# Weight tiles of three opening groups parked or subtracted on VectorE, the state decay on ScalarE, and parking during a down projection

## The chip, the cores and the metric

The kernel runs on one core of one Trainium2 chip. The metric is device time in microseconds: 1893.84 us, the median of three runs (1893.59 to 1896.18). TensorE is called PE below, VectorE DVE, ScalarE ACT, GpSimd POOL, and SyncE, which issues the DMAs, SP.

## The reference

One inference step of a two-layer decoder for a prompt of 512 tokens and a sample group of 8 sequences of one token each, 520 tokens together, width 1024, all in float32:

```python
m = hybrid_mixer(rmsnorm(x, norm_mix_pre[0]), ...)   # layer 0: dilated attention and an SSD scan
m = gdn_mixer(rmsnorm(x, norm_mix_pre[1]), ...)      # layer 1: gated DeltaNet
x = x + rmsnorm(m, norm_mix_post[l])
f = swiglu(rmsnorm(x, norm_ffn_pre[l]), w_gate, w_up, w_down)   # (silu(h @ w_gate) * (h @ w_up)) @ w_down
x = x + rmsnorm(f, norm_ffn_post[l])
```

The DeltaNet input weight has 48 column tiles of 128 (tiles 0 to 7 are q, 8 to 15 k, 16 to 31 v, 32 to 47 z) and 32 more columns for two gates. The FFN has 2816 hidden columns, 22 tiles. For each sample sequence and each of 16 heads DeltaNet also returns the new state `s * g + outer(k, u)`, a 128 x 128 matrix.

## The kernel before

Activations lie transposed, features on partitions and the 520 tokens along the free dimension, in two halves of 256 and 264. A float32 product is made of three matmuls per k-tile and half: high part of the weight with high part of the activation, the same with the activation's low part, and the weight's low part with the activation's high part (`lin`, L327). `WStream.split` (L172) makes the two parts of a unit of four k-tiles by 128 columns: a cast of the raw weights gives `whi`, on ACT (L317) or, at every `hi_v`th unit, on DVE (L318), and raw less high gives `wlo` (L193), on POOL at every `lo_pool`th unit and on DVE otherwise. `lo_pool = 1` puts all on POOL, 0 none. Raw weights come in loads of 1 MB, 256 columns of eight k-tiles or 128 columns of sixteen, into two buffers; `whi` and `wlo` have four each.

While the first FFN runs its gate and up tiles, units of the DeltaNet weight are **parked**: `park` (L152) loads a unit of 256 KB, casts it on ACT, subtracts on POOL and stores the low part to DRAM, each call doing one of these steps for three successive units. Later `split` fetches a parked low part by DMA (`wlo<-pk`) and subtracts nothing; the high part is cast again. The list (`PTILES`) holds tiles 10 to 15, 0 to 7 and 16 to 21, forty units, and there are forty calls, two to a pair of tiles for the gate and two for the up, from pair 1 on; two more calls drain the last units.

Each stage ends in `out_proj` (L497): eight output tiles, the last ones by halves. Then the residual and the norm of the new activations go half by half: for each of eight feature tiles DVE multiplies the mixer's output with R (L302, tiles `p` or `bm`), adds it to the residual stream, and ACT and DVE make the high part (`Hh`; in DeltaNet `Hl`) and the low part (`Hl`; in DeltaNet `bm`, L309) of the scaled sum. So that PE has work as soon as half 0 of a feature tile is there, the next stage opens with `group` (L336): several column tiles at once, half 0 first. In the FFNs these are gate tiles 0 and 1 and up tiles 0 and 1, eight units of which the up tiles' lie outside the rings (`p` in the first, `b` and `cs` in the second); in DeltaNet the 32 gate columns, tile 8 and tile 9 (in `cs`). `out_proj` leaves `lo_pool = 1`, so POOL makes these low parts.

In the second FFN, between the tiles, `state_steps` (L1867) updates the sample's states, four heads at a time in 32 steps: SP loads a state of 128 x 512 into `cs` and a broadcast row `b<-ud`, POOL multiplies it by its decays (L302, `cs<-cs,small`), DVE adds the outer product in two instructions (L309, `cs<-b,CS,cs`), and two steps on SP stores it. A pair of tiles takes four steps, beginning with pair 1. In that stage DVE multiplies the gate's sums by the norm (`sq<-acc,R`), ACT applies Silu (into `acc` or `small`), DVE multiplies with the up tile (`sq<-acc` or `sq<-small,acc`), ACT casts the product and DVE makes its low part. `sq` has three buffers, the accumulators four.

The program text gives what is issued; a scheduler settles each engine's order, in which loads and casts of weights and evictions have high priority, and engines and DMA queue then work strictly in that order.

Of the kernel before, what the change touches and what calls it, by code (L numbers as in the profile page):

```python
# [13 lines left out]
ALU = mybir.AluOpType  # L14
# [13 lines left out]
KF = FF // 128  # L28
# [90 lines left out]
 'yd': 'G'}  # L119


PTILES = [*range(10, 16), *range(8), *range(16, 22)]


def KN(n, v, *others):
# [6 lines left out]
class WStream:  # L132
# [19 lines left out]
    def park(s, ins):  # L152

        k = s.k
        with k.tc.issue_after(ins), k.tc.issue_after(k.last_load):
            done, new = s.wait
            s.wait = [None, None]
            if done:
                d = k.dr.tile([128, 4, 128], F32, tag="pk%d" % len(s.parked), name="pk%d" % len(s.parked))
                k.dma(d, done[2].bitcast(F32))  # L160
                s.parked[done[0]] = d
            if new:
                k.cp("A", new[2], new[1])
                k.tt(new[2], new[1], new[2].bitcast(F32), ALU.subtract, k.nc.gpsimd)
                s.wait[0] = new
            if s.todo:
                ap, c0, k0 = s.todo.pop(0)
                q = len(s.todo) % 2
                raw, lo = k.B("cs", 1040 + 512 * q, 4, 128), k.B("b4", 2080 + 512 * q, 4, 128, dt=F32R)
                k.dma(raw, ap[k0 * 128:(k0 + 4) * 128, c0:c0 + 128].rearrange("(k p) c -> p k c", p=128))  # L170
                s.wait[1] = (ap.tensor.name, ap.offset, c0, k0), raw, lo
# [37 lines left out]
            for j in range(4):  # L209
                yield kts[k0] + j, hi[:, j], lo[:, j]  # L210

    def rows(s, ap, c0, loads):

        for k0, n, offs in loads:
            raw = s.load(ap, k0, n, c0, 128)
            for o in offs:
                m = min(4, n - o)
                hi, lo = s.split(raw, o, m, 0)
                for j in range(m):
                    yield k0 + o + j, hi[:, j], lo[:, j]  # L220


class Ker:
# [112 lines left out]
    def group(s, w, xh, xl, nkt):  # L336

        w = [list(v) for v in w]
        ps = [{} for _ in w]
        for t in range(len(w)):  # L340
            if t % 2 == 0:
                a = s.acc()
            ps[t][0] = a[:, 256 * (t % 2):256 * (t % 2) + 256]
        for t in range(len(w)):
            ps[t][1] = (s.acc() if t < 2 else s.mx())[:, 0:HW[1]]
        for h in (0, 1):
            for t, v in enumerate(w):
                s.lin(v, xh, xl, nkt, (h,), ps[t])
        return ps

    def lnexp(s, ins):
# [145 lines left out]
    def out_proj(s, rows, xh, xl, nkt, mp, n, l, pre, tail=2, final=False):  # L497

        s.mp, s.sqs = mp, ([], [])
        if not final:  # L500
            tail = KN("tail%d%d" % (n, l), tail, 2, 3, 4)

        def evac(ps, ot):
            ins = None
            with s.tc.high_priority():
                for h in ps:
                    if ot == 7:
                        s.sqs[h].append(s.tms(HW[h]))
                        ins = s.act(s.sqs[h][0], ps[h], AF.Square)
                    if ot == 7 and final and h:  # L510
                        s.ts(mp[:, ot, HALF[h]], ps[h], s.gain(n, l, ot))
                    else:
                        s.act(mp[:, ot, HALF[h]], ps[h], scale=s.gain(n, l, ot))
                    if ot < 7:
                        s.add_sq(h, ps[h], ot == 0, s.tmp)
            return ins

        for ot in range(8 - tail):
            evac(s.lin(rows(ot), xh, xl, nkt), ot)
            if final and ot == 2:  # L520
                s.final_early()
        s.lo_pool = KN("lp_t%d%d" % (n, l), 2, 1, 3, 4)
        for h in (0, 1):
            for ot in range(8 - tail, 8):
                ins = evac(s.lin(rows(ot), xh, xl, nkt, (h,)), ot)
            if h == 0:
                with s.tc.issue_after(ins):
                    s.nc.scalar.preload_act_table_set("natural_log_exp_and_others")
                if final:
                    s.final_first()  # L530
                else:
                    s.pre = pre()
                    s.prenorm(*s.pre, 0, s.residual(n == 3, 0))
        if final:
            s.final_last()
        s.lo_pool, s.hi_v = 1, 0

    def spill(s):
        s.xd = s.dr.tile([128, KD * NT], F32, tag="xd", name="xd", bufs=2)
# [547 lines left out]
    def ffn(s, l):  # L1087
        nc = s.nc
        g, u, d = s.i["w_ffn_gate"][l], s.i["w_ffn_up"][l], s.i["w_ffn_down"][l]
        order = ["b4", "p0", "X", "p7"] + (["bm", "p2"] if l == 0 else ["p2", "bm"])  # L1090
        s.gen(*(("b4", "p0") if l == 0 else ("b4", "cs")))
        x = s.lay("Hh"), s.lay("Hl")

        def hid(w):
            def f(k, h):
                sl = 2 * k + w
                if sl < 4:
                    return s.B("b4", sl * NT, NT, dt=F32R)[:, HALF[h]]
                n, sl = order[1 + (sl - 4) // 8], (sl - 4) % 8
                return s.layh(n)(sl, h)  # L1100
            return f

        hh, hl = hid(0), hid(1)
        spare = lambda on: {h: s.mx("ma")[:, 0:HW[h]] for h in (0, 1)} if on else None
        kts = list(range(8))
        ax = [("p0", 1024 * q) for q in range(4)] if l == 0 else [("b4", 0), ("b4", 1024), ("b4", 2048), ("cs", 1040)]
        first = s.group([s.W.tile(g, 128 * t, kts) for t in (0, 1)] +
                        [s.W.tile(u, 128 * t, kts, out=ax[2 * t:2 * t + 2]) for t in (0, 1)], *x, 8)
        s.gen("p2" if l == 0 else "bm")
        if l == 0:  # L1110
            w = s.i["w_gdn_in"][0]
            s.copy_every = 0
            s.W.todo = [(w, 128 * t, k0) for t in PTILES for k0 in (0, 4)]
        s.lo_pool = KN("lp_f%d" % l, 1, 2, 3)
        s.hi_v = KN("hv_f%d" % l, 0, 2, 3, 4, 1)
        if l:
            s.gen("cs")
            s.new_small()
            sgs = s.small(NT)
            states = s.state_steps()  # L1120
        for p in range(11):
            sg = {}
            for t in (2 * p, 2 * p + 1):
                ps = first[t] if p == 0 else s.lin(s.W.tile(g, 128 * t, kts), *x, 8, ps=spare(t < 2 + KN("ma_f%d" % l, 0, 1, 2)))
                for h in (0, 1):
                    sl = (s.B("cs", NT * (t % 2), NT) if l == 0 else sgs if t % 2 else s.accT)[:, HALF[h]]
                    gt = s.tmp(HW[h])
                    with s.tc.high_priority():
                        s.tt(gt, ps[h], s.R2[:, HALF[h]], ALU.mult)
                    with s.tc.issue_after(s.norm_ins):  # L1130
                        ins = s.act(sl, gt, AF.Silu)
                    sg[t, h] = sl
                if l == 0 and p:
                    s.W.park(ins)
                if l and p:
                    next(states, None)
            for t in (2 * p, 2 * p + 1):
                ps = first[2 + t] if 2 + t < len(first) else s.lin(s.W.tile(u, 128 * t, kts), *x, 8)
                for h in (0, 1):
                    gt = s.tmp(HW[h])  # L1140
                    with s.tc.high_priority():
                        s.tt(gt, sg[t, h], ps[h], ALU.mult)
                    a = hh(t, h)
                    ins = s.act(a, gt)
                    s.tt(hl(t, h), gt, a.bitcast(F32), ALU.subtract)
                if l == 0 and p:
                    s.W.park(ins)
                if l and p:
                    next(states, None)
        for _ in states if l else ():  # L1150
            pass
        while l == 0 and s.W.wait != [None, None]:
            s.W.park(ins)
        s.gen("Hh")
        s.lo_pool = KN("lp_d%d" % l, 1, 2, 3)
        s.hi_v = KN("hv_d%d" % l, 0, 2, 3, 4, 1)
        s.out_proj(lambda ot: s.W.rows(d, ot * 128, [(0, 16, (0, 4, 8, 12)), (16, 6, (0, 4))]), hh, hl, KF,
                   s.B("Hh", 0, KD, NT), 3, l, lambda: (0, 1, s.lay("Hl"), s.layh("bm")), final=l == 1)

    def cache_shift(s):  # L1160
# [706 lines left out]
    def state_steps(s):  # L1867

        i, o = s.i, s.o
        dap = lambda d: d if isinstance(d, bass.AP) else d[:]  # L1870
        ud = dap(s.ud)
        gb = s.small(8, 2, 16)
# [5 lines left out]
        for n in range(4 * NS + 2):  # L1878
            with s.tc.issue_after(s.last_load):
                if n > 1:  # L1880
                    s.dma(state(o["sgs"], n - 2), S(n - 2))
                if 0 < n < 4 * NS + 1:
                    t, (b, h) = S(n - 1), at(n - 1)
                    s.tt(t, t, gb[:, b, 0, h].unsqueeze(2).to_broadcast([128, 4, 128]), ALU.mult, s.nc.gpsimd)
                    for j in range(2):
                        v = slice(2 * j, 2 * j + 2)
                        s.stt(t[:, v], ub(n - 1)[:, v], s.kqs[:, h.start // 2 + j, b, 0:1], t[:, v], ALU.mult, ALU.add)
                if n < 4 * NS:
                    b, h = at(n)
# [51 lines left out]
```

## Time and profile before

| | |
|---|---|
| median of three runs | 1893.84 us |
| profiled execution | 1886.62 us, its span 1884.8 us, 1.8 us around it |
| PE / DVE / POOL / ACT busy | 1744.3 / 1160.9 / 890.8 / 769.3 us |
| mean granted PE clock | 0.966 |
| first FFN: opening; gate, up and down | 434 to 475; to 803 |
| last tiles of the first down projection, by halves | 803 to 845 |
| DeltaNet: opening; body; z and output projection | 845 to 900; to 1300; to 1440 |
| second FFN: opening; with state steps; rest and down | 1440 to 1521; to 1670; to 1783 |
| end | 1783 to 1884.8 |

Times inside the span are of that one profiled execution, which was 7.2 us shorter than the median. A row of a timeline has start, duration, engine, line, operation, output<-inputs, shape, count, and in square brackets how long the engine was idle before it and what ended that. A row of the table of windows has the stretch and its length, then busy time and instruction count of PE, weight loads, DVE, ACT and POOL, the granted clock, the DMA engines' busy share and GB/s.

### The profile page before, as it was taken

What the parts mean: (1) busy time and instruction counts of PE and PEld (TensorE: products, weight loads), DVE (VectorE), ACT (ScalarE), POOL (GpSimd) and SP (SyncE); (2) the same over time, 40 slices, a digit from 0 to 9 for tenths busy, and PEclk for the clock granted to TensorE, in tenths of its full rate; (3) what the DMA queues carried; (4) which work ended last, traced back from release to release, by engine and by line L of the source; (5) the groups of instructions that cost most, each with busy time, mean ns of one, the idle gap of its engine ahead of it and who ended that gap; (6) DMA issues with size and microseconds to landing.
All of it is one profiled execution on the core that took longest, in us unless ns stands there. A gap on an engine that the chain in (4) does not pass through costs nothing.

```text
span 1884.8 us, 36666 instructions
## 1 busy us (share of the span) xinstructions
PE 1744.3 (93%) x14263; PEld 1656.7 (88%) x14263; DVE 1160.9 (62%) x2325; ACT 769.3 (41%) x1868; POOL 890.8 (47%) x793
## 2 busy tenths in 40 slices
PE   7889999898999999989977888989999999999996
PEld 6878777598999999978977887888998999999995
DVE  6898879539433331168799967788703866753025
ACT  5432235555433333346765655644435311111222
POOL 2565657234666663342342564544557333323452
PEclk9999999898999999999988999999999999999998
DMA  7336766354556553346753113246435588863554
GB/s 258 129 126 184 221 193 179 130 154 126 157 182 189 185 175 100 92 141 212 245 172 112 43 45 110 60 125 186 135 91 180 160 257 262 262 206 123 160 160 152
DMA packets 328784, 300.39 MB, mean 159 GB/s; under 512 B 14529, under 2 KB 299910, under 8 KB 327442
## 3 DMA queue, kind: packets, MB, share of 16 engines
q1 hardware_dynamic: 327958, 297.37, 50.7%
q8 instruction: 112, 1.84, 0.4%
q10 hardware_dynamic: 652, 0.68, 0.1%
q14 instruction: 62, 0.51, 0.1%
HBM read 261.98 MB, written 72.52 MB: 177 GB/s over the span
## 4 chain that ended last, share of the span: by engine, by line
PE 50%; DVE 18%; DMA 9%; ACT 4%; issue 4%; POOL 2%; SPq 1%; DVEq 0%; ACTq 0%; POOLq 0%
PE acc L296 43%; PE ma L296 4%; DVE p L302 3%; DVE cs L309 3%; PE mb L296 2%; DMA b<-ud 2%; DMA raw<-in_w_ffn_down_dram 1%; DVE wlo L193 1%; ACT L312 1%; DMA cs<-in_state_gdn_dram 1%; POOL cs L302 1%; SPq L324 1%; DVE b L302 1%; DVE Hl L309 1%; PE mb L299 1%
## 5 line engine op out<-in xcount | busy, mean ns | idle before, releaser
L193 POOL TENSOR_TENSOR wlo<-raw,whi 128x512 fp32r<-128x512 f32 (+2 forms) x342 | 453.2, 1328 | 504.9 <-ACT whi L317 304.3
L296 PE MATMUL acc<-Hl,whi 128*128 128x256 f32 (+1 forms) x2576 | 561.4, 291 | 29.7 <-DVE cs L302 18.1
L296 PEld LDWEIGHTS acc<-Hl,whi 128*128 128x128 f32 x2576 | 419.2, 193 | 43.8 <-issue 18.8
L317 ACT CAST whi<-raw 128x512 fp32r<-128x512 f32 (+3 forms) x392 | 234.3, 603 | 436.2 <-PE acc L296 335.5
L296 PE MATMUL acc<-Hh,whi 128*128 128x256 f32 (+1 forms) x1824 | 390.2, 289 | 9.6 <-DVE sq L302 6.3
L296 PE MATMUL acc<-Hh,wlo 128*128 128x256 f32 (+1 forms) x1824 | 389.7, 289 | 1.2 <-DVE wlo L193 1.2
L296 PEld LDWEIGHTS acc<-Hh,whi 128*128 128x128 f32 x1824 | 293.6, 192 | 17.2 <-DVE sq L302 9.2
L296 PEld LDWEIGHTS acc<-Hh,wlo 128*128 128x128 f32 x1824 | 293.4, 192 | 9.0 <-issue 6.7
L296 PE MATMUL acc<-bm,whi 128*128 128x256 f32 (+1 forms) x1136 | 234.8, 290 | 0.1
L296 PE MATMUL acc<-p,whi 128*128 128x264 f32 (+1 forms) x1280 | 226.4, 284 | 0.0
L193 DVE TENSOR_TENSOR wlo<-raw,whi 128x512 fp32r<-128x512 f32 (+1 forms) x141 | 117.6, 835 | 140.3 <-ACT whi L317 137.7
L296 PEld LDWEIGHTS acc<-p,whi 128*128 128x128 f32 x1280 | 187.8, 190 | 0.8 <-DVE p L302 0.5
L296 PEld LDWEIGHTS acc<-bm,whi 128*128 128x128 f32 x1136 | 181.1, 193 | 2.8 <-issue 2.1
L318 DVE CAST whi<-raw 128x512 fp32r<-128x512 f32 x131 | 65.4, 503 | 179.8 <-PE acc L296 136.4
L296 PE MATMUL acc<-Hl,wlo 128*128 128x256 f32 (+1 forms) x752 | 169.7, 295 | 1.2 <-DMA wlo<-pk 0.7
L296 PE MATMUL acc<-p,wlo 128*128 128x256 f32 (+1 forms) x704 | 162.0, 284 | 7.1 <-DVE wlo L193 7.1
L296 PEld LDWEIGHTS acc<-Hl,wlo 128*128 128x128 f32 x752 | 126.1, 196 | 3.9 <-issue 1.6
L296 PEld LDWEIGHTS acc<-p,wlo 128*128 128x128 f32 x704 | 117.4, 189 | 8.0 <-DVE wlo L193 7.9
L296 PE MATMUL acc<-X,whi 128*128 128x264 f32 (+1 forms) x512 | 99.1, 288 | 1.1 <-ACT X L312 1.1
L309 DVE SCALAR_TENSOR_TENSOR cs<-cs,cw 128x512 f32<-128x512 f32 x100 | 90.4, 905 | 12.0 <-POOL cs L302 7.0
L302 POOL TENSOR_TENSOR cs<-cs,small 128x512 f32<-128x512 f32 x48 | 55.1, 1152 | 87.8 <-DMA cs<-in_state_gdn_dram 68.8
L296 PEld LDWEIGHTS acc<-X,whi 128*128 128x128 f32 x512 | 79.3, 193 | 2.4 <-ACT X L312 2.2
(466 smaller groups left out, 2989.6 us busy)
## 6 DMA issues: line engine op xcount, KB each, us to landing
raw<-in_w_gdn_in_dram SPq DMA_DIRECT2D x24, 1024.0 KB
raw<-in_w_ffn_gate_dram SPq DMA_DIRECT2D x22, 1024.0 KB
raw<-in_w_ffn_up_dram SPq DMA_DIRECT2D x22, 1024.0 KB
raw<-in_w_ffn_down_dram SPq DMA_DIRECT2D x20, 1024.0 KB
raw<-in_w_hyb_in_dram SPq DMA_DIRECT2D x16, 1024.0 KB
out_sv_dram<-in_cache_attn_v_dram SPq DMA_DIRECT2D x16, 1023.0 KB
out_sk_dram<-in_cache_attn_k_dram SPq DMA_DIRECT2D x16, 1023.0 KB
cs<-in_w_gdn_in_dram SPq DMA_DIRECT2D x40, 256.0 KB
```

What stands on the lines that cost most here:

```text
L193: eng.tensor_tensor(out=lo[:, :nk, d:d + n], in0=raw[:, :, o:o + n], in1=hi[:, :nk, d:d + n].bitcast(F32), op=ALU.subtract)
L296: s.nc.tensor.matmul(out, lhsT=lhsT, rhs=rhs, start=start, stop=stop, skip_group_check=skip)
L299: s.nc.tensor.transpose(out, in_, s.ident[0:in_.shape[0], 0:in_.shape[0]])
L302: return (eng or s.nc.vector).tensor_tensor(out=out, in0=a, in1=b, op=op).ins
L309: return s.nc.vector.scalar_tensor_tensor(out=out, in0=a, scalar=sc, in1=b, op0=op0, op1=op1).ins
L312: return s.nc.scalar.activation(out=out, in_=in_, func=f, **kw).ins
L317: return s.nc.scalar.copy(out, in_).ins
L318: return (s.nc.vector if e == "V" else s.nc.gpsimd).tensor_copy(out, in_).ins
L324: return (eng or s.nc.sync).dma_start(out=out, in_=in_).ins
```

## The change

Five things change. The list of parked units becomes tiles 8 to 15 and 0 to 7 of the DeltaNet weight, then gate tiles 0 and 1 and up tiles 0 and 1 of the second FFN, then tiles 16 to 22 of DeltaNet: 54 units. The forty calls in the first FFN's gate and up take the first forty; the last 14 and the draining are done in the first down projection, where `rows` calls `park` three times per output tile. `out_proj` leaves `lo_pool = 0`, so low parts of an opening group that are not parked are made by DVE. `group` takes half 1 k-tile by k-tile over all column tiles instead of column tile after column tile. The state steps begin with pair 2 of the second FFN. The decay of a state step is done by ACT in four instructions of 128 x 128, each with the head's decay as its scale.

```diff
-PTILES = [*range(10, 16), *range(8), *range(16, 22)]
+PTILES = [*range(8, 16), *range(8)]
+DTILES = [*range(16, 23)]
...
     def park(s, ins):
 
         k = s.k
-        with k.tc.issue_after(ins), k.tc.issue_after(k.last_load):
+        with k.after(ins), k.tc.issue_after(k.last_load):
...
-    def rows(s, ap, c0, loads):
+    def rows(s, ap, c0, loads, steps=False):
...
                 for j in range(m):
                     yield k0 + o + j, hi[:, j], lo[:, j]
+                if steps and o % 8 == 4:
+                    s.park(None)
...
-        for h in (0, 1):
+        for t, v in enumerate(w):
+            s.lin(v, xh, xl, nkt, (0,), ps[t])
+        for n in range(nkt):
             for t, v in enumerate(w):
-                s.lin(v, xh, xl, nkt, (h,), ps[t])
+                kt, hi, lo = v[n]
+                for lhs, x, st, sp in ((hi, xh, n == 0, False), (hi, xl, False, False), (lo, xh, False, n == nkt - 1)):
+                    s.mm(ps[t][1], lhs, x(kt, 1), st, sp)
...
-        s.lo_pool, s.hi_v = 1, 0
+        s.lo_pool, s.hi_v = 0, 0
...
-            s.W.todo = [(w, 128 * t, k0) for t in PTILES for k0 in (0, 4)]
+            s.W.todo = ([(w, 128 * t, k0) for t in PTILES for k0 in (0, 4)] +
+                        [(s.i[n][1], 128 * t, k0) for n in ("w_ffn_gate", "w_ffn_up") for t in (0, 1) for k0 in (0, 4)] +
+                        [(w, 128 * t, k0) for t in DTILES for k0 in (0, 4)])
...
-                if l and p:
+                if l and p > 1:
                     next(states, None)
...
-        while l == 0 and s.W.wait != [None, None]:
-            s.W.park(ins)
...
-        s.out_proj(lambda ot: s.W.rows(d, ot * 128, [(0, 16, (0, 4, 8, 12)), (16, 6, (0, 4))]), hh, hl, KF,
+        s.out_proj(lambda ot: s.W.rows(d, ot * 128, [(0, 16, (0, 4, 8, 12)), (16, 6, (0, 4))], l == 0 and ot < 6), hh, hl, KF,
...
-                    s.tt(t, t, gb[:, b, 0, h].unsqueeze(2).to_broadcast([128, 4, 128]), ALU.mult, s.nc.gpsimd)
+                    for j in range(4):
+                        s.act(t[:, j], t[:, j], scale=gb[:, b, 0, h.start + j:h.start + j + 1])
```

**DVE in the opening of the first FFN**, from the first low part of half 0's activations on (`Hl`; `p_74` is the mixer's output, `p_75` the residual stream, `rs` half 1's norm). Before:

```order
L309 SCALAR_TENSOR_TENSOR Hl<-p_75,par,Hh 128x256
L302 TENSOR_TENSOR p_74<-p_74,R_4695 128x256
L309 SCALAR_TENSOR_TENSOR Hl<-p_75,par,Hh 128x256 x2
L302 TENSOR_TENSOR p_74<-p_74,R_4695 128x256
L302 TENSOR_TENSOR p_75<-p_75,p_74 128x256
L309 SCALAR_TENSOR_TENSOR Hl<-p_75,par,Hh 128x256
L302 TENSOR_TENSOR p_75<-p_75,p_74 128x256
L309 SCALAR_TENSOR_TENSOR Hl<-p_75,par,Hh 128x256
L302 TENSOR_TENSOR p_74<-p_74,R_4695 128x256
L302 TENSOR_TENSOR p_75<-p_75,p_74 128x256
L306 TENSOR_SCALAR rs_4908<-mb 128x264
```

After:

```order
L312 SCALAR_TENSOR_TENSOR Hl<-p_75,par,Hh 128x256
L305 TENSOR_TENSOR p_74<-p_74,R_4695 128x256
L194 TENSOR_TENSOR wlo<-raw,whi 128x512
L312 SCALAR_TENSOR_TENSOR Hl<-p_75,par,Hh 128x256 x2
L305 TENSOR_TENSOR p_74<-p_74,R_4695 128x256
L305 TENSOR_TENSOR p_75<-p_75,p_74 128x256
L194 TENSOR_TENSOR wlo<-raw,whi 128x512
L312 SCALAR_TENSOR_TENSOR Hl<-p_75,par,Hh 128x256 x2
L305 TENSOR_TENSOR p_74<-p_74,R_4695 128x256
L194 TENSOR_TENSOR wlo<-raw,whi 128x512
L305 TENSOR_TENSOR p_75<-p_75,p_74 128x256
L194 TENSOR_TENSOR wlo<-raw,whi 128x512
```

Four subtractions of weights (L194) now stand among the instructions that make half 0's `Hl`; four more, of the up tiles, follow a few rows later, ahead of the last two `Hl`.

**POOL in the opening of the second FFN**, from the residual's last two products on (`wlo` a ring's low part, `b` and `cs` the up tiles' low parts, `ex` half 0's and 1's kept norm). Before:

```order
L193 TENSOR_TENSOR wlo<-raw,whi 128x512
L302 TENSOR_TENSOR acc<-acc,sq 128x264
L193 TENSOR_TENSOR wlo<-raw,whi 128x512 x4
L193 TENSOR_TENSOR b_16798<-raw,b_16798 128x512 x3
L193 TENSOR_TENSOR cs<-raw,cs 128x512
L306 TENSOR_SCALAR ex<-rs_16756 128x256
L193 TENSOR_TENSOR wlo<-raw,whi 128x512 x2
L306 TENSOR_SCALAR ex<-rs_16789 128x264
L302 TENSOR_TENSOR cs<-cs,small 128x512 x4
```

After:

```order
L194 TENSOR_TENSOR wlo<-raw,whi 128x512
L305 TENSOR_TENSOR acc<-acc,sq 128x264
L309 TENSOR_SCALAR ex<-rs_16826 128x256
L194 TENSOR_TENSOR wlo<-raw,whi 128x512
L309 TENSOR_SCALAR ex<-rs_16859 128x264
L194 TENSOR_TENSOR wlo<-raw,whi 128x512 x30
```

The eight subtractions of the opening are gone, and the states' decays with them. The up tiles' four low parts are fetched on SP (`cs<-pk`, three `b<-pk`) between the sample's last state load in DeltaNet and the store of its accumulator; the gate tiles' four (`wlo<-pk`) stand there two behind the opening's first load of gate weights and a cache copy, two behind its first load of up weights.

**ACT in the second FFN beside the state steps**, one pair of tiles (`acc` and `small` are the two gate tiles' Silu, `X` the up tile's high part). Before:

```order
L312 ACTIVATE acc<-sq 128x256
L312 ACTIVATE acc<-sq 128x264
L312 ACTIVATE small<-sq 128x256
L312 ACTIVATE small<-sq 128x264
L312 ACTIVATE X<-sq 128x256
L312 ACTIVATE X<-sq 128x264
```

After:

```order
L315 ACTIVATE acc<-sq 128x256
L315 ACTIVATE acc<-sq 128x264
L315 ACTIVATE cs<-cs,small 128x128 x4
L315 ACTIVATE small<-sq 128x256
L315 ACTIVATE small<-sq 128x264
L315 ACTIVATE cs<-cs,small 128x128 x4
L315 ACTIVATE X<-sq 128x256
L315 ACTIVATE X<-sq 128x264
L315 ACTIVATE cs<-cs,small 128x128 x8
```

Four decays of a step stand between the two gate tiles' Silu, four before the first up tile's cast, and eight, two steps, before the second's.

More of the change, by code (lines that the diff above doesn't have):

```diff
@@ L1147, in ffn @@
                     s.W.park(ins)
-                if l and p:
+                if l and p > 1:
                     next(states, None)
```

## The prediction

> **What bounds the kernel now.** I read the page first, then the table by stage, and only then the timelines of the stages in which TensorE waits. From the page, the row of TensorE and the shares of the chain that ended last:
>
> ```profile
> PE 1744.3 (93%) x14263; PEld 1656.7 (88%) x14263; DVE 1160.9 (62%) x2325; ACT 769.3 (41%) x1868; POOL 890.8 (47%) x793
> ...
> PE 50%; DVE 18%; DMA 9%; ACT 4%; issue 4%; POOL 2%; SPq 1%; DVEq 0%; ACTq 0%; POOLq 0%
> ```
>
> TensorE is busy 93% of the span, so only 140 us of idle time and some slow stretches can be won at all; DVE is next on the chain. The table by stage shows where they lie (window; then busy us and count for PE, weight loads, DVE, ACT, POOL; granted clock; DMA share; GB/s):
>
> ```profile
> 434.00:457.00 23.00, 17.17 (x107) 15.43 (x106) 22.93 (x41) 13.44 (x33) 11.42 (x9) 0.78 0.52 159
> 475.00:803.00 328.00, 328.00 (x2731) 327.99 (x2730) 98.39 (x174) 114.58 (x243) 185.90 (x147) 1.00 0.51 154
> 728.00:804.00 76.00, 75.70 (x628) 75.29 (x626) 9.61 (x16) 24.08 (x51) 25.93 (x25) 1.00 0.35 96
> 845.00:900.00 55.00, 50.73 (x398) 49.22 (x398) 48.15 (x105) 31.77 (x68) 14.89 (x20) 0.97 0.62 206
> 1446.00:1470.00 24.00, 19.52 (x117) 17.57 (x117) 22.00 (x39) 13.64 (x32) 13.59 (x10) 0.79 0.52 175
> 1486.00:1500.00 14.00, 10.05 (x68) 9.58 (x68) 12.93 (x26) 4.91 (x11) 7.14 (x6) 0.88 0.88 287
> 1521.00:1670.00 149.00, 145.34 (x1183) 142.75 (x1182) 102.62 (x206) 18.76 (x51) 48.07 (x42) 1.00 0.82 266
> ```
>
> The second row is the steady state: 2731 matmuls in 328 us, 0.12 us each, no gap. Against it a stage loses its length less 0.12 us per matmul. The opening of the first FFN (434 to 457): 23 - 107 x 0.12 = 10.2 us. The opening of DeltaNet (845 to 900): 55 - 47.8 = 7.2. The opening of the second FFN: 24 - 14.0 = 10.0 and then 14 - 8.2 = 5.8 at 1486 to 1500. In the first FFN opening DVE is busy 22.93 of 23 us: it, not the weights, sets the pace. The stage with the state steps (1521 to 1670) has 3.7 us of PE idle time, the first down projection (728 to 804) 0.3. So the change can win in three openings, some 33 us in all, and hardly anywhere else.
>
> **The change part by part.** Why DVE is slow in the openings, on DVE's timeline of the first FFN (start, duration, instruction):
>
> ```profile
> 434.43 1.49 DVE L302 TENSOR_TENSOR p<-p,R 128x256 f32<-128x256 f32 x1
> 435.85 2.90 DVE L309 SCALAR_TENSOR_TENSOR Hl<-p,par,Hh 128x256 fp32r<-128x256 f32 x2
> 438.67 1.50 DVE L302 TENSOR_TENSOR p<-p,R 128x256 f32<-128x256 f32 x1
> ...
> 440.42 0.47 DVE L309 SCALAR_TENSOR_TENSOR Hl<-p,par,Hh 128x256 fp32r<-128x256 f32 x1
> 440.82 0.41 DVE L302 TENSOR_TENSOR p<-p,p 128x256 f32<-128x256 f32 x1
> ...
> 442.68 4.08 DVE L309 SCALAR_TENSOR_TENSOR Hl<-p,par,Hh 128x256 fp32r<-128x256 f32 x3
> 446.68 1.51 DVE L302 TENSOR_TENSOR rs<-rs,rs 128x264 f32<-128x264 f32 x1
> ```
>
> and on POOL's of the same stretch:
>
> ```profile
> 434.19 5.69 POOL L193 TENSOR_TENSOR wlo<-raw,whi 128x512 fp32r<-128x512 f32 x4
> 442.36 5.54 POOL L193 TENSOR_TENSOR p<-raw,p 128x512 fp32r<-128x512 f32 x4 [2.48 <-ACT p L317]
> ```
>
> The same Hl takes 0.47 us (next start after 0.40) between POOL's two groups and about 1.4 us beside them. Beside the first group DVE does 4 instructions in 5.7 us where 4 x 0.37 = 1.5 would do, beside the second 4 in 5.5: lost 4.2 + 4.0 = 8.2 us over 11.2 us of POOL, 0.73 us per us.
>
> *First FFN opening.* The eight subtractions move from POOL to DVE; the 8.2 us go. What one costs on DVE is to be read in the second opening, with the next start 0.61 us on:
>
> ```profile
> 1492.46 0.68 DVE L193 TENSOR_TENSOR wlo<-raw,whi 128x512 fp32r<-128x512 f32 x1
> 1493.07 0.41 DVE L318 CAST whi<-raw 128x512 fp32r<-128x512 f32 x1
> ```
>
> 8 x 0.61 = 4.9 us on the same busy engine, so 3.3 net; I take 3. Bounds: 6 if the last four stand behind what PE waits for (8.2 less 4 x 0.61), 0 if a subtraction waiting for ACT's cast holds up an Hl each time. Half 1 by row tiles: the order of before already mixed the tiles, so 0, with up to 1 us either way inside these bounds.
>
> *DeltaNet opening.* Two of its three tiles, 8 and 9, are parked, so four subtractions of POOL and their pace on DVE go:
>
> ```profile
> 843.22 1.49 DVE L309 SCALAR_TENSOR_TENSOR R<-rs,rs 128x264 f32<-128x264 f32 x1
> 844.75 2.84 DVE L302 TENSOR_TENSOR Hh<-Hh,R 128x264 f32<-128x264 f32 x2
> 847.51 1.49 DVE L302 TENSOR_TENSOR p<-p,Hh 128x264 f32<-128x264 f32 x1
> 848.92 0.42 DVE L302 TENSOR_TENSOR Hh<-Hh,R 128x264 f32<-128x264 f32 x1
> ```
>
> Four instructions in 5.7 us, at 0.34 each alone 1.4: 4.3 us. PE feels less of it, and the chain of waits then has a parked low part:
>
> ```profile
> 849.60 0.51 PE L296 MATMUL acc<-Hl,whi 128*128 128x264 f32 x2 [2.00 <-ACT Hl L312]
> ```
> ```profile
> 856.91 7.97 DMA wlo<-pk
> ```
>
> A parked low part can take 8 us to land, and now tile 8's two come by DMA too, behind the opening's raw weights on SP. The 2.0 us wait goes, and some of what follows it: 2.5; bounds 0 (the transfer is late) and 4.3.
>
> *Second FFN opening.* All eight units are parked; POOL's subtractions go and no one takes them over:
>
> ```profile
> 1447.89 2.89 POOL L193 TENSOR_TENSOR wlo<-raw,whi 128x512 fp32r<-128x512 f32 x2
> 1452.59 3.21 POOL L193 TENSOR_TENSOR wlo<-raw,whi 128x512 fp32r<-128x512 f32 x2 [1.81 <-ACT whi L317]
> 1458.68 4.16 POOL L193 TENSOR_TENSOR b<-raw,b 128x512 fp32r<-128x512 f32 x3 [2.88 <-ACT b L317]
> 1462.80 1.48 POOL L193 TENSOR_TENSOR cs<-raw,cs 128x512 fp32r<-128x512 f32 x1
> ```
> ```profile
> 1460.97 0.72 DVE L302 TENSOR_TENSOR rs<-rs,rs 128x264 f32<-128x264 f32 x1 [1.96 <-ACT rs L312]
> ```
>
> DVE waits itself for 2.0 of these 11.7 us, so 9.7 x 0.73 = 7.1 us at most come off its chain. The state steps start a pair later and their decay leaves POOL, so what follows goes as well:
>
> ```profile
> 1485.97 3.42 POOL L302 TENSOR_TENSOR cs<-cs,small 128x512 f32<-128x512 f32 x3
> ```
> ```profile
> 1491.14 0.39 PE L296 MATMUL acc<-Hh,whi 128*128 128x256 f32 x1 [2.74 <-DVE sq L302]
> 1493.20 0.81 PE L296 MATMUL acc<-Hh,wlo 128*128 128x256 f32 x2 [1.22 <-DVE wlo L193]
> ```
>
> PE's waits there are 2.74 + 1.22 = 4.0 us. Together 11.1 at most. Against it: the gate tiles' four low parts now come by DMA in the ring wlo, which the output projection holds until the stage begins (about 1446); with the 8 us of above they may land at 1454, and POOL had them at 1450.8 and 1455.8 (the ends of the first two rows). I take 7; bounds 2 (half of the waits at 1491 alone) and 11.1. A step's three transfers on SP move a pair later with it; 34 of 36 turns are used, so they end a pair later too, before the down projection: 0, bounds -1 and 0.
>
> Here a page of the Trainium skill bears on the size. PE runs at a granted 0.79 over 1446 to 1470: 0.21 x 24 = 5 us of the 10.0. "TensorE: Matmul & The Clock Gate", section "What's actually happening", says that one window of some 3.4 us of sustained work opens the clock fully; by that rule, were PE fed without gaps, only 0.5 x 3.4 = 1.7 us of the 5 would be left, an estimate, and the sum would be about 3 us lower. I don't take it, since the operands will still arrive one Hl at a time.
>
> *State steps.* From the groups of the page, of this stretch by form, and of ACT:
>
> ```profile
> L302 POOL TENSOR_TENSOR cs<-cs,small 128x512 f32<-128x512 f32 x48 | 55.1, 1152 | 87.8 <-DMA cs<-in_state_gdn_dram 68.8
> ```
> ```profile
> L309 DVE SCALAR_TENSOR_TENSOR cs<-b,CS,cs 128x256 f32<-128x256 f32 x48 | 28.1, 623 | 39.4 <-POOL cs L302 22.3 <-DMA b<-ud 17.1
> ```
> ```profile
> L312 ACT ACTIVATE X<-X,small 128x128 f32<-128x128 f32 x32 | 10.0, 390 | 3.4 <-POOL X L302 3.4
> ```
>
> 32 POOL instructions of 1.15 us become 128 on ACT of about 0.39: 1.56 us a step, 50 us on an engine that is busy 18.76 of 149 us here. A step gets 0.4 us longer, DVE is freed of POOL's company, and PE has 3.7 us of waits to give back. I take 1; bounds -3 and 3.7; a heavier loss is rival A.
>
> *Parking in the first down projection.* 14 units: ACT 14 x 0.6, POOL 14 x 1.3 = 18 us, and 7 MB of DMA in 76 us at a DMA share of 0.35. PE's gap there is 0.3 us; ACT and POOL are busy a third. What hides it is that slack; if it fails, raw weights queue behind stores on SP. I take -0.5; bounds -3 and 0.
>
> *Four parked low parts (1 MB) ahead of the sample's accumulator* on SP in DeltaNet: -1; bounds -3 and 0 (1 MB at the 206 GB/s of the DeltaNet row above is 5 us, a part of it hidden).
>
> Sum: 3 + 2.5 + 7 + 1 - 0.5 - 1 = 12.0 us. The profiled execution took 1886.62 us, 7.2 below the median of 1893.84; from it the sum gives 1874.6, from the median 1881.8, and the median is what I predict. A difference under 0.2% (3.8 us) can't be told from none here.
>
> **The rivals.** *A, slower: ACT stands behind the states' transfers.* ACT takes its instructions in order, and four decays stand between the two gate tiles' activations, eight between the up tiles' casts. POOL waited for the state transfers so:
>
> ```profile
> POOL cs L302 <- DMA cs<-in_state_gdn_dram: 68.8, 23, 7.1
> ```
>
> 3 us on average, up to 7.1; moved to ACT, the wait holds the activations, these hold three sq buffers, and DVE then cannot empty the accumulators. With 7.1 + 1.6 us the delay comes to 8.7, and a tile's 48 matmuls are 5.8 us: it decides where two tiles (11.6 us) no longer cover the delay plus DVE's own queue. At 2 us a pair over nine pairs that is 18 us, less the 11 won elsewhere: 1901. Against it: ACT has slack of that length before its casts; in this stretch it waits for DVE 8 us each time (31.7 in 4, the longest 10.3):
>
> ```profile
> ACT X L312 <- DVE sq L302: 31.7, 4, 10.3
> ```
>
> *B, half the gain: the parked low parts land late.* With transfers like the 7.97 us one, the DeltaNet opening gives 0 and the second FFN's only the 1486 part, 3: 3 + 3 + 1 - 1.5 = 5.5, 1888. For it: the ring that comes free late. Against it: four of the eight are loaded long before.
>
> *C, no change.* PE's order in the openings is set by DVE's chain of Hl, which stays; if the subtractions that DVE takes over, and delays in DeltaNet, cost what POOL's leaving gives, 10 of the 12 go: 1892. For it: DVE is at 22.93 of 23 us. That the change does not take place is no case: the order shows it.
>
> **How the numbers follow.** Forecast 0.57, B 0.19, C 0.13, A 0.11. Faster: the forecast and nearly all of B, 0.75; same 0.13; slower 0.12. The range: from the forecast with its three openings near their upper bounds (12 + 9, some clock with it: 1872) to C and a light A (1895).
>
> **What would show it.** In the changed profile the Hl of the first FFN opening should take 0.47 us, not 1.4; POOL should have no subtraction of an opening's tiles from 1447 on, the wait of 2.74 us for sq gone and the granted clock of the second opening above 0.79; PE's idle time in the state stage at or below 3.7 us with ACT near 69 us there. It is wrong if PE waits for wlo<-pk for more than 2 us in an opening (B), if sq waits in the state stage sum to over 8 us with ACT waiting for the states' transfers (A), or if the openings keep their 33 us (C).

## The result, and the profile after

Four runs of the changed kernel took 1866.83 us in the median (1864.42 to 1872.44), four of the kernel before 1894.27: a ratio of 0.9858, interval 0.9834 to 0.9881. Timed again in more rounds (below) the ratio was 0.9868, 0.9850 to 0.9886. So the change is worth some 25 us. The forecast was 12 us, 1881.8, with a range from 1872 to 1895: the measured time lies some 5 us below the range.

The profiled execution after took 1864.42 us, its span 1862.6. Since everything shifts, stages are compared by their length between the same instructions: the DVE instruction `R<-rs,rs` that ends each norm, and two loads of an activation table on ACT. All times are from the timelines; "again" is a second profiled execution of the same kernel.

| stage | before | again | after | again |
|---|---|---|---|---|
| opening of the first FFN (mixer's norm of half 0 to token norm of half 1) | 45.7 | 47.0 | 41.6 | 41.5 |
| its gate, up and down, to the first residual norm | 347.9 | 349.4 | 348.9 | 350.1 |
| down's last halves and DeltaNet's opening, to the table load at its gates | 55.7 | 52.2 | 49.4 | 48.5 |
| DeltaNet, to the norm of half 0 at its end | 566.2 | 570.3 | 568.0 | 570.9 |
| opening of the second FFN, to the token norm of half 1 | 46.3 | 46.3 | 38.1 | 38.1 |
| the rest of it, to the last table load | 357.4 | 359.8 | 353.2 | 353.5 |

In the means 4.9 us are won in the first opening, 5.0 around DeltaNet's, 8.2 in the second FFN's and 5.2 behind it; 0.8 are lost beside the parking in the down projection and 1.2 in DeltaNet; the remaining 2 us of 23.5 lie before 427 us, where only the order of layer 0's own group differs, and at the end, where nothing does. These 2 us are no gain that can be told from none: in all the changed kernels below the first opening begins between 422.9 and 428.5 us. The stages as windows of the profile after (the columns are those of the prediction's table):

```profile
432.00:452.00 20.00, 16.68 (x112) 15.04 (x112) 20.00 (x50) 13.54 (x33) 0.42 (x1) 0.91 0.60 183
723.00:799.00 76.00, 75.42 (x623) 74.80 (x621) 13.56 (x16) 28.11 (x60) 40.71 (x35) 1.00 0.55 159
838.00:890.00 52.00, 51.62 (x419) 50.62 (x419) 45.11 (x105) 32.95 (x72) 11.45 (x18) 0.99 0.70 233
1436.00:1460.00 24.00, 21.15 (x163) 19.71 (x161) 21.71 (x56) 17.08 (x42) 2.38 (x3) 1.00 0.64 215
1500.00:1650.00 150.00, 148.22 (x1220) 146.77 (x1219) 90.67 (x205) 48.27 (x144) 21.92 (x17) 1.00 0.82 261
```

In DeltaNet's opening PE (TensorE) now does 419 matmuls in 52 us, 1.7 us above 0.12 us each, where before it was 7.2. In the second FFN's first 24 us it does 163 where it did 117, so by the same count 4.4 us are lost there, not 10.0, and POOL works 2.4 us there where it worked 13.6; the granted clock is 1.00, not 0.79. In the state stage PE is idle 1.8 us of 150, where it was 3.7 of 149. DVE (VectorE) in the first FFN's opening:

```profile
433.56 0.87 DVE L312 SCALAR_TENSOR_TENSOR Hl<-p,par,Hh 128x256 fp32r<-128x256 f32 x2
434.35 0.42 DVE L305 TENSOR_TENSOR p<-p,R 128x256 f32<-128x256 f32 x1
434.69 0.42 DVE L305 TENSOR_TENSOR p<-p,p 128x256 f32<-128x256 f32 x1
435.02 0.69 DVE L194 TENSOR_TENSOR wlo<-raw,whi 128x512 fp32r<-128x512 f32 x1
```

Two Hl take 0.87 us, where they took 2.90, and the subtraction behind them costs its 0.6 to the next start. In the second FFN's opening, SP's issue of the parked low parts, and all that PE waited for from 1430 to 1480 (total, times, longest):

```profile
1434.11 1.78 SPq L327 DMA_DIRECT2D wlo<-pk  x2
...
1437.96 2.35 SPq L327 DMA_DIRECT2D wlo<-pk  x2
```
```profile
PE acc L299 <- DVE Hl L312: 1.6, 4, 0.5
PE acc L299 <- ACT Hh L315: 1.2, 1, 1.2
PE acc L299 <- DVE wlo L194: 0.4, 1, 0.4
```

No wait for a parked low part is among them, and the waits of 2.74 and 1.22 us at 1491 have shrunk to one of 0.43, at 1474. ACT in the state stage, its waits from 1480 to 1665 and its decays from 1500 to 1650:

```profile
ACT cs L315 <- DMA cs<-in_state_gdn_dram: 73.8, 29, 8.3
```
```profile
L315 ACT ACTIVATE cs<-cs,small 128x128 f32<-128x128 f32 x96 | 30.8, 391 | 60.8 <-DMA cs<-in_state_gdn_dram 60.7
```

ACT (ScalarE) now takes over POOL's (GpSimd's) wait for the states, up to 8.3 us, just as rival A says, but PE does not feel it: its idle time there has shrunk. A decay takes 0.391 us, four in a row 1.28 (each starts before the one ahead has ended), less than the 1.56 that the forecast took for a step.

### The profile page after: what moved, and what is told of

The parts are those of the page before. It is cut to its first block, busy times and chain, and to the rows that moved or that the text cites. A ratio compares the mean times of both kernels' runs of the same rounds, so it can differ in the third digit from the quotient of the medians.

```text
span 1862.6 us, 36877 instructions
## 1 busy us (share of the span) xinstructions
PE 1733.5 (93%) x14263; PEld 1649.1 (89%) x14263; DVE 1135.7 (61%) x2336; ACT 814.9 (44%) x2010; POOL 839.3 (45%) x750
## 5 line engine op out<-in xcount | busy, mean ns | idle before, releaser
L194 POOL TENSOR_TENSOR wlo<-raw,whi 128x512 fp32r<-128x512 f32 (+1 forms) x327 | 434.1, 1330 | 560.3 <-ACT whi L320 262.3
L194 DVE TENSOR_TENSOR wlo<-raw,whi 128x512 fp32r<-128x512 f32 (+2 forms) x148 | 122.9, 833 | 131.1 <-ACT whi L320 129.1
L305 POOL TENSOR_TENSOR b<-cs,b 128x512 fp32r<-128x512 f32 x54 | 75.6, 1400 | 32.8 <-ACT b L320 31.6
```

The costliest lines, as they stand in the source:

```text
L194: eng.tensor_tensor(out=lo[:, :nk, d:d + n], in0=raw[:, :, o:o + n], in1=hi[:, :nk, d:d + n].bitcast(F32), op=ALU.subtract)
L305: return (eng or s.nc.vector).tensor_tensor(out=out, in0=a, in1=b, op=op).ins
```

## The experiments

Theory **T**: DVE is slow beside POOL's subtractions, and the openings gain because this company is gone. Theory **W**: they gain because the work itself is gone from them, whoever did it. Theory **S**: the gain comes from the states, which start later and are scaled on ACT. Single executions of before ran from 1883 to 1902 us, so each kernel is given by its median, its ratio to the kernel before timed beside it, with the interval, and its distance to after from the ratios (1 in 1000 is 1.9 us).

| run | median | ratio (interval) | against after |
|---|---|---|---|
| after2 | 1868.0 | 0.9868 (0.9850 to 0.9886) | |
| x_lo1 | 1871.8 | 0.9888 (0.9862 to 0.9914) | +3.8 |
| x_nopark | 1874.3 | 0.9894 (0.9869 to 0.9920) | +4.9 |
| x_company | 1878.4 | 0.9913 (0.9893 to 0.9933) | +8.5 |
| x_both | 1887.0 | 0.9966 (0.9950 to 0.9982) | +18.5 |
| x_poolstate | 1872.9 | 0.9885 (0.9868 to 0.9903) | +3.2 |
| x_group | 1869.2 | 0.9869 (0.9855 to 0.9884) | +0.2 |
| x_p1 | 1871.9 | 0.9883 (0.9856 to 0.9910) | +2.8 |
| x_nodown | 1867.6 | 0.9870 (0.9840 to 0.9901) | +0.4 |
| x_t11 | 1866.9 | 0.9862 (0.9834 to 0.9890) | -1.1 |
| x_f1lo0 | 1865.2 | 0.9855 (0.9827 to 0.9882) | -2.5 |
| x_best | 1864.5 | 0.9853 (0.9835 to 0.9870) | -2.8 |
| x_best2 | 1868.3 | 0.9876 (0.9853 to 0.9898) | +1.5 |

Only x_company and x_both lie clear of after's interval. For the others the times alone settle nothing, and the argument rests on the length of the stage that the edit touches, against its length in kernels that are alike in that stage.

**The two kernels again.** No edit.

> The kernel before once more, unchanged. Both theories expect a ratio of 1.000 within 0.002. What it is for: the first profiled execution of before was 7.2 us shorter than its median, the one of after 2.4 us. If a second profile of before shows a stage that is some 5 us longer than in the first, that stage varies from run to run and 5 of the 27 us lie there; if it is again near 1886, an execution under the profiler and the others differ, or the chips do.

> After once more, unchanged, timed in more rounds, since single executions of before ran from 1883 to 1902. All theories: a ratio between 0.984 and 0.988. It gives the base for the other runs and a second profile of each stage.

Before against itself gave 1.0006 (0.9987 to 1.0025); its profiled execution took 1892.41 us, 5.8 more than the first. The table of stages shows where: +1.3 and +1.5 in the first FFN, +4.1 in DeltaNet, +2.4 in the last stage, -3.5 around DeltaNet's opening, while the second FFN's opening repeats to 0.01 us. No one stage holds the difference: the first profile was a quick execution. DeltaNet alone differs by 4 us between the two.

**The low parts of the first opening back on POOL.**

```diff
-        s.lo_pool, s.hi_v = 0, 0
+        s.lo_pool, s.hi_v = 1, 0
```

> After, but out_proj leaves lo_pool = 1 again, so POOL and not DVE makes the eight low parts of the first FFN's opening (and DeltaNet's two small ones); all else as in after. Theory T (DVE is slow beside POOL's subtractions, and the gain of the openings is that this company is gone): the first FFN's Hl take 1.4 us again, that opening loses 4 us against after, about 1871. Theory W (the gain is work that is no longer done in the openings, whoever did it): DVE is freed of eight subtractions of 0.6 us, so no loss or a gain, 1862 to 1867.

3.8 us slower, and that opening is 45.6 us long, 4.1 more than in after and 2.9 more than in any kernel below that leaves its low parts to DVE (41.5 to 42.7). Its other stages lie within what the changed kernels spread by. DVE's and POOL's timelines there are before's again:

```profile
431.11 2.90 DVE L312 SCALAR_TENSOR_TENSOR Hl<-p,par,Hh 128x256 fp32r<-128x256 f32 x2
...
437.94 4.08 DVE L312 SCALAR_TENSOR_TENSOR Hl<-p,par,Hh 128x256 fp32r<-128x256 f32 x3
```
```profile
429.45 5.69 POOL L194 TENSOR_TENSOR wlo<-raw,whi 128x512 fp32r<-128x512 f32 x4
```

DVE has eight instructions less to do and is slower: W falls for this opening.

**Nothing parked for the openings.**

```diff
-PTILES = [*range(8, 16), *range(8)]
-DTILES = [*range(16, 23)]
+PTILES = [*range(10, 16), *range(8), *range(16, 22)]
+DTILES = [22]
...
-                        [(s.i[n][1], 128 * t, k0) for n in ("w_ffn_gate", "w_ffn_up") for t in (0, 1) for k0 in (0, 4)] +
```

> After, but DeltaNet's tiles 8 and 9 and the second FFN's gate and up tiles 0 and 1 are not parked (the list is before's with tile 22 added, so only two units are parked in the first down projection): DVE makes these twelve low parts in the openings, beside no POOL subtraction. T: 4 x 0.6 us more on DVE in DeltaNet's opening and 8 x 0.6 us in the second FFN's, 7 us at most, 1869 to 1874, and no Hl above 0.6 us. W: the 5.7 us of DeltaNet's opening and the 11 of the second FFN's are lost again: about 1883.

4.9 us slower. The stage of DeltaNet's opening is 50.7 us long, 1.7 more than after's mean; the second FFN's opening 40.6, 2.5 more. What this says is seen against x_both below, which has these low parts on POOL and the state steps as late as here. Its two stages are 54.2 and 42.4 us long. So with DVE subtracting, 3.5 of the 5.2 us stay in DeltaNet's opening, but only 1.8 of 4.3 in the second FFN's. Within the latter, from the norm R of half 0 to that of half 1, the stretch takes 21.2 us with POOL subtracting (before and x_both), 17.6 here and 14.6 in after: there T and W are worth about as much as each other. DVE's timeline and the window of the second opening:

```profile
1452.08 0.68 DVE L194 TENSOR_TENSOR wlo<-raw,whi 128x512 fp32r<-128x512 f32 x1
1452.68 0.47 DVE L312 SCALAR_TENSOR_TENSOR Hl<-p,par,Hh 128x256 fp32r<-128x256 f32 x1
...
1459.50 1.26 DVE L312 SCALAR_TENSOR_TENSOR Hl<-p,par,Hh 128x256 fp32r<-128x256 f32 x3
```
```profile
1446.00:1470.00 24.00, 19.38 (x135) 17.66 (x134) 24.00 (x57) 15.17 (x37) 3.14 (x3) 0.93 0.52 176
```

DVE is busy all 24 us, no Hl takes more than 0.48, and half of eight times 0.6 us reaches the stage. W expected 1883 and T 1869 to 1874; it is 1874.3.

**POOL company that nobody needs.** Eight subtractions on POOL in the second FFN's opening, of constants into a buffer that is overwritten unread (the diff leaves out a line that keeps the constants at hand).

```diff
+        if l:
+            du = s.B("p7", 3648, 512, dt=F32R)
+            with s.after(s.res_ins):
+                for _ in range(8):
+                    s.tt(du, s.cst[:, 0:512], s.cst[:, 128:640], ALU.subtract, nc.gpsimd)
```

> After, with eight subtractions of 128 x 512 added on POOL in the opening of the second FFN, from a constant into a buffer that nobody reads before it is overwritten: nothing waits for them and the work of after is unchanged. T: DVE loses 0.7 us per us of them, 11 us of POOL cost 6 to 8 us of that opening: 1873 to 1875, with Hl or p at 1.1 to 1.5 us there and PE's granted clock there below 1.00. W: nobody waits for them, so 1867.

8.5 us slower, and the opening is 47.8 us long, longer than before's 46.3. POOL's, DVE's and PE's timelines, and the window:

```profile
1444.20 11.14 POOL L305 TENSOR_TENSOR p<-cst 128x512 fp32r<-128x512 f32 x8 [1.55 <-PE acc L299]
```
```profile
1447.10 1.48 DVE L312 SCALAR_TENSOR_TENSOR Hl<-p,par,Hh 128x256 fp32r<-128x256 f32 x1
1448.50 1.48 DVE L305 TENSOR_TENSOR bm<-bm,R 128x256 f32<-128x256 f32 x1
1449.91 1.48 DVE L312 SCALAR_TENSOR_TENSOR Hl<-p,par,Hh 128x256 fp32r<-128x256 f32 x1
1451.31 1.49 DVE L305 TENSOR_TENSOR bm<-bm,R 128x256 f32<-128x256 f32 x1
1452.73 1.48 DVE L305 TENSOR_TENSOR p<-p,bm 128x256 f32<-128x256 f32 x1
```
```profile
1451.44 0.58 PE L299 MATMUL acc<-Hl,whi 128*128 128x256 f32 x1 [5.00 <-DVE Hl L312]
```
```profile
1440.00:1464.00 24.00, 14.54 (x81) 12.31 (x80) 22.01 (x33) 11.63 (x28) 13.23 (x11) 0.79 0.62 212
```

Nothing waits for these eight, and yet DVE does one instruction every 1.4 us while they last, just one for each of POOL's (11.14 / 8 = 1.39). PE waits 5.0 us for an Hl, and its clock over those 24 us is 0.79, as in before. This shows T directly, at more than the 6 to 8 us that T expected.

**All three openings as before.** The edits of x_lo1 and x_nopark together.

> After without the parking of the opening's units and with lo_pool = 1: all three openings have their subtractions on POOL as before; state decay on ACT, state steps from pair 2, group by row tiles and parking of tiles 16 to 21 stay. Theory T (DVE's company): the three openings lose 4 + 5.7 + 7 of the gain, less what the later state steps keep of the second FFN's: 1880 to 1886. Theory S (the gain comes from the later start of the state steps and the decay on ACT): most of the gain stays, 1870.

18.5 us slower, 1 us more than T's range; 6.4 us of the gain (0.34% of before) stay for the states and the rest. S, which expected 1870, falls as the main cause. Alone, the two edits cost 3.8 and 4.9: what comes on top, 9.8 us, is that the low parts which x_nopark gives to DVE are POOL's here. By the stages, 3.5 of it lie in DeltaNet's opening and 1.8 in the second FFN's; the rest is not located.

But S holds a good part of the second opening. It is 42.4 us long, not 46.3, so 3.9 of the 8.2 us won there are the states' absence, and 4.3 the subtractions'. All 3.9 lie between the opening's last two norms (4.2 us here, 8.1 in before). There before shows company again, the decays of the state steps on POOL at 1485.97 beside DVE:

```profile
1486.00 1.29 DVE L302 TENSOR_TENSOR rs<-rs,rs 128x264 f32<-128x264 f32 x1 [1.08 <-ACT rs L312]
1487.33 1.16 DVE L309 SCALAR_TENSOR_TENSOR rs<-rs,rs 128x264 f32<-128x264 f32 x1
1488.41 1.26 DVE L309 SCALAR_TENSOR_TENSOR cs<-b,CS,cs 128x256 f32<-128x256 f32 x1
```

**The state decay back on POOL**, from pair 2 on.

```diff
-                    for j in range(4):
-                        s.act(t[:, j], t[:, j], scale=gb[:, b, 0, h.start + j:h.start + j + 1])
+                    s.tt(t, t, gb[:, b, 0, h].unsqueeze(2).to_broadcast([128, 4, 128]), ALU.mult, s.nc.gpsimd)
```

> After, but the state decay is one POOL instruction of 128 x 512 a step again, from pair 2 on. T: the decay's place is worth little, since PE waits 3.7 us in all in the state stage of before and 2.0 in after: 1867 to 1870. S: it carries a good part, 1875 or more. Against both, A (ACT's wait for the states holds its activations): 1865 or less.

3.2 us slower by the ratios, 4.9 by the medians, between what T and S expected. The stage behind the second opening is 356.0 us long, 2.7 more than after's, though x_nopark and x_both, which do there what after does, have 355.8 and 356.5. Its window, and the state's update on DVE from 1521 to 1670 (after: 504 ns):

```profile
1500.00:1650.00 150.00, 146.20 (x1194) 143.95 (x1193) 102.79 (x207) 18.96 (x50) 49.15 (x41) 1.00 0.82 265
```
```profile
L312 DVE SCALAR_TENSOR_TENSOR cs<-b,CS,cs 128x256 f32<-128x256 f32 x48 | 29.8, 661 | 39.9 <-POOL cs L305 21.2 <-DMA b<-ud 18.7
```

PE is idle 3.8 us there, about as in before (3.7 of 149), and 1.8 in after; in the kernels that do there what after does it is 0 to 2.6. So PE waits less with the decays on ACT, longer and blocked as its queue is, than with them on POOL; that the whole kernel gains by it is not shown.

**The states from pair 1 again**, decay on ACT: `p > 1` back to `p` in both places.

> After, but the state steps begin with pair 1 of the second FFN again, the decay staying on ACT. It splits what the stage from that opening's last norm to the end gained (some 4 to 6 us) between start and place of the decay; with the decay back on POOL that stage lost 2.7 us of it. T (DVE's company): the states' two DVE instructions and waits for transfers come into the opening again, 1 to 3 us: 1869 to 1871. S (the later start is what matters): 1872 or more.

2.8 us slower; the opening is 42.7 us long, 4.6 more than after's, the stage behind it 351.1, 2.3 less (within what that stage spreads by, 350.1 to 356.5). So the later start alone, with the decay on ACT, is worth about as much to the opening as x_both says. DVE's timeline shows how the states get in the norm's way, here by DVE's waiting for ACT's decays ahead of it:

```profile
1477.41 1.07 DVE L312 SCALAR_TENSOR_TENSOR cs<-b,CS,cs 128x256 f32<-128x256 f32 x2 [1.08 <-ACT cs L315]
1478.89 0.48 DVE L312 SCALAR_TENSOR_TENSOR cs<-b,CS,cs 128x256 f32<-128x256 f32 x1 [0.41 <-ACT cs L315]
...
1482.91 0.43 DVE L312 SCALAR_TENSOR_TENSOR R<-rs,rs 128x264 f32<-128x264 f32 x1
```

**The group's order on PE as before** (the loop over halves in `group` restored), and **nothing parked in the down projection** (the last list of `todo` empty).

> After, but group takes half 1 column tile by column tile as before. All theories: no difference that can be told from none (within 3 us of after), since the order on PE differs in few rows.

> After without the second list: nothing is parked in the first down projection, and tiles 16 to 22 make their low parts in DeltaNet on POOL. The prediction put the parking in the down projection at -0.5 us (bounds -3 and 0). If it costs that, the stretch from the first FFN's last norm to the first residual of the down projection is 0.5 to 1 us shorter than after's; what DeltaNet then loses, with 14 more subtractions of POOL in a stretch bound by several engines, is 0 to 4 us: 1867 to 1871.

Neither can be told from after (+0.2 and +0.4 us). Without the parking, the first FFN behind its opening is 348.9 us long, 0.6 less than after's mean, and DeltaNet some 3 us longer: what it costs and what it saves lie within what two executions differ by.

**Less of POOL elsewhere.** `lp_t11` 2 instead of 1; `lp_f1` 0 instead of 3; both; both and DVE for all residual products of half 0.

```diff
- 'lp_t11': 1,
+ 'lp_t11': 2,
...
- 'lp_f1': 3,
+ 'lp_f1': 0,
...
-            pool = k % KN("upd%d" % h, 4, 3, 8, 2) == KN("updo", 3, 1, 2, 0)
+            pool = h and k % KN("upd%d" % h, 4, 3, 8, 2) == KN("updo", 3, 1, 2, 0)
```

> After, but in the halves at the end of DeltaNet's output projection every second low part is made by DVE instead of all by POOL. T: POOL's subtractions still stand beside DVE's norm and first products there (rs 1.40, p<-p,bm 3.39 for five), two to four fewer of them would free 1 us each, less 0.6 us for each on DVE: 0 to 2 us faster, 1866 to 1868. W: more work for the engine that sets the pace: 1869.

> After, but in the gate and up tiles of the second FFN no low part is made by POOL (a third was). T: POOL is empty there, DVE does some 29 subtractions more (0.6 us each, 17 us of its 50 idle ones in the state stage) but every instruction of it takes its time alone; PE waits 2.0 us there in after: 0 to 2 us faster, 1866 to 1868. Rival: DVE's queue becomes the bound and sq comes late: 1870 or more.

> After with both edits that a profile showed useful in a stage: no low part on POOL in the second FFN's gate and up tiles, and every second one on DVE at the end of DeltaNet's output projection. T: the gains of the two stages add, 2.5 us in the stretch after the second FFN's opening and 1 to 2 before it: 1864 to 1866. Rival (each is noise): 1867 to 1869.

> The same, and the two products per residual of half 0 that POOL makes (bm<-bm,R in the second FFN's opening, p<-p,R in the first's) go to DVE as well, so that no POOL instruction stands beside DVE's chain from the norm to the first Hl. T, by one DVE instruction held for each POOL instruction: 2 x 1 us come free and 2 x 0.35 are added in each opening, 1 us faster an opening: 1861 to 1865. Rival W (two instructions more on the engine that sets the pace): 1866 to 1868.

x_t11 can't be told from after. x_f1lo0 is 2.5 us faster by the ratios, within the interval; its stage behind the opening is 2.5 us shorter (350.9), and with POOL empty PE is idle 0.8 us of 150. But x_nodown, where POOL is busy 22.5 us of these 150, has 350.1 us and 0.7: neither figure shows that the empty POOL did it.

```profile
1500.00:1650.00 150.00, 149.21 (x1232) 148.15 (x1231) 97.38 (x227) 49.23 (x146) 0.00 (x0) 1.00 0.84 269
```

x_best has the lowest median of all, 1864.5, as forecast; it beats before for certain, after by 2.8 us within the intervals, so that the two gains add is not shown. x_best2 was expected faster and is not: in its first opening it wins 1.0 us (41.8 against x_best's 42.7, no more than that opening spreads by in kernels that are alike there, 41.5 to 42.7), in its second it loses 2.1. There DVE comes to the first Hl 4.6 us after R (1437.23 to 1441.85), in after 5.9, and something else is last. A piece of the chain that ended last, and ACT's and PE's timelines:

```profile
1440.99 8.37 DMA raw<-in_w_ffn_up_dram
```
```profile
1449.38 1.66 ACT L320 CAST b<-raw 128x512 fp32r<-128x512 f32 x3 [3.78 <-DMA raw<-in_w_ffn_up_dram]
```
```profile
1450.05 0.39 PE L299 MATMUL acc<-Hh,b 128*128 128x256 f32 x1 [4.01 <-ACT b L320]
```

The raw up weights, issued on SP at 1440.99 between the first of the parked low parts and the other three, land 8.4 us later (5.2 in x_best). ACT, waiting to cast them, holds up the last high parts of the activations behind them. So in this kernel the second opening's bound is a transfer; why it took longer than in x_best stays open.

## Why the prediction was wrong

The mechanism and the places were right, and the sizes were not. The forecast of 12 us was half of what came, since the terms of the three openings were taken well below the bounds worked out for them; the largest miss is the second FFN's, 7 us taken and 11.7 measured.

- *The first opening* was put at 3, bounds 0 and 6; it gave 4.9 in the profiles, and x_lo1 loses 4.1 of that opening. Right in kind, a little small: if all 8.2 us of company came free, the eight subtractions on DVE cost the stage 3.3 us and not the 4.9 charged for them.
- *DeltaNet's opening* was put at 2.5, bounds 0 and 4.3; it gave 5.0 together with the down projection's last halves. The two executions of before differ by 3.5 there, but x_both repeats it, 5.2 above after. The failing step is "PE feels less of it": PE felt all of it. The late transfer of 7.97 us that was feared does not show as a wait of PE.
- *The second opening* was put at 7, bounds 2 and 11.1. It gave 8.2, and the waits at 1491, 4.0 us, shrank to 0.4 right behind it: 8.2 + 3.5 = 11.7, a little above its upper bound. This is the largest error. Counted over the opening and all behind it, with the one execution of x_both between, 7.5 us are the subtractions' (the forecast's plain count was 7.1) and 6.0 the states'. Two steps failed. "They may land at 1454": issued at 1434 and 1438, the gate tiles' parked low parts kept nobody waiting. And the clock was set aside: it was granted in full. In before PE was busy 0.67 us of the three from 1449 to 1452, and the clock granted from 1452 to 1460 was 0.51; after the change PE was busy 1.79 us or more of every three to four from 1436 to 1446, and the clock stayed at 1.00, so all of the 0.21 x 24 = 5 us came back. A page of the Trainium skill had given 3 us for it, "TensorE: Matmul & The Clock Gate", section "What's actually happening", by which a short window of sustained work opens the clock; the trace gave more, since here the clock never closed. The "operands will still arrive one Hl at a time" was true and did not matter: PE waited four times for an Hl, 0.5 us at most.
- The sum of 0.73 us for each us of POOL was near: in x_company 11.1 us of POOL cost 9.7 us of that opening, 0.87, and DVE's own loss there, 8 instructions in 11.1 us where 3 us would do, is 0.73.
- *The state stage* was put at 1, bounds -3 and 3.7; of the 5.2 us won behind the opening 3.5 are the waits at 1491, 1.7 are left. x_poolstate and x_p1 put the decay's place at 2.7 and the later start at 2.3 net, sizes within what that stage spreads by in kernels that are alike there.
- *Parking in the down projection* (-0.5) and *DeltaNet's sample* (-1) came out at -0.8 and -1.2, sizes that two executions of one kernel can differ by.
- *Rival A* was refuted though its first half came true: ACT waits 73.8 us for states, and PE's waits for sq in the state stage are 1.8 us in all. *B* was refuted by PE's waits, none of them for a parked low part. *C* was refuted by the windows of the three openings.
- The range ended at 1872, the three openings near their bounds; the four upper bounds, 6 + 4.3 + 11.1 + 3.7, add up to 25.1 us, about the result. That is in part chance, since the first opening and the states gave less than theirs. What was called a bound was in the main the plain count, and the forecast a discount on it for dangers that did not come.

What stays open: how much of DeltaNet's term is the opening and how much the halves before it, the small terms inside the spread of single executions, and what the states' later start and the decay's place are each worth to the whole kernel.

## What to carry to other kernels

Where VectorE feeds TensorE at a stage's start, count each two-input GpSimd instruction that runs beside it as one VectorE instruction held up, even if nothing depends on it; work moved onto the busy engine can be cheaper than work beside it. When a count gives a bound, forecast near the count, and let a danger that the trace does not show as a wait widen the range only. And where TensorE's waits at a stage's start shrink, count the clock that can come back as well: here it was 5 of the 24 us.

## What the hardware showed

A POOL instruction with two SBUF inputs (128x512) held one DVE instruction for its whole length: some 1.40 us from start to start instead of 0.34 to 0.40, for tensor_tensor and for scalar_tensor_tensor with two SBUF inputs (x_company above). In the state stage of before a cast was held as well, beside a decay on POOL (1604.55, 1.12 us long):

```profile
1604.70 1.26 DVE L318 CAST whi<-raw 128x512 fp32r<-128x512 f32 x1
1606.06 0.69 DVE L193 TENSOR_TENSOR wlo<-raw,whi 128x512 fp32r<-128x512 f32 x1
```

(the same cast takes 0.42 us elsewhere). DVE instructions that read one operand from PSUM were not held where the trace shows both: in the same stage two of them ran wholly beside a POOL subtraction at their usual 0.75 us, and the subtraction of DVE's own behind them was held:

```profile
1593.37 1.29 POOL L193 TENSOR_TENSOR wlo<-raw,whi 128x512 fp32r<-128x512 f32 x1 [4.20 <-DVE whi L318]
```
```profile
1593.40 0.75 DVE L302 TENSOR_TENSOR sq<-acc,R 128x256 f32<-128x256 f32 x2
1594.07 1.14 DVE L193 TENSOR_TENSOR wlo<-raw,whi 128x512 fp32r<-128x512 f32 x1
```

The Trainium skill's page "GPSIMD Engine Reference", section "1. Specifications", names such a contention, with VectorE instructions that have two SBUF inputs or work in a 2-port mode; the rows with two inputs agree, 1.40 us against 0.34 to 0.40. Whether the cast ran in such a mode no row here shows.
